# Expert matrices of a mixture-of-experts trunk loaded whole into two neighbouring slots instead of in two halves

## The chip, the cores and the metric

The kernel runs on one core of a Trainium2 chip. The metric is the device time of one execution in microseconds (us). The core has TensorE (PE, matrix products), VectorE (DVE), ScalarE (ACT), GpSimd (POOL) and SyncE (SP); SP only issues DMAs here. Sixteen DMA engines carry what the core reads and writes.

## What is computed

A trunk of two layers over 512 tokens of width 1024, all in float32. Layer 0 mixes tokens with a forgetting attention, layer 1 with a causal pooling; each is followed by a mixture of 32 experts, of which a token uses two. Every sub-layer has its RMS norm and is modulated by a vector that comes from `c` and the matrices `ada_w`. What matters here is the expert part:

```python
def grouped_moe(h, router_w, router_bias, w1, w3, w2):
    ...
    e_idx = top_k(where(e_mask, sel, -inf), 2)   # two experts of the best group
    ...
    def expert_block(args):
        xb, e = args
        return (silu(xb @ w1[e]) * (xb @ w3[e])) @ w2[e]
    ...
for i in range(2):
    mod = silu(c) @ ada_w[i] + ada_b[i]
    x = x + gt_m * mixer_i(modulate(rmsnorm(x), sh_m, sc_m))
    x = x + gt_f * grouped_moe(modulate(rmsnorm(x), sh_f, sc_f), ...)
```

Each of the 32 experts has w1 and w3 (1024 x 512) and w2 (512 x 1024): three matrices of 2 MB (2 x 1,048,576 bytes), so 192 MB a layer.

## The kernel before

**Passes.** A layer's experts run in 13 passes of up to 128 token places. A pass holds one to four experts: 2, 2, 4, 2, 2, 2, 1, 4, 2, 2, 3, 2, 4 in the order of passes 0 to 12 (`PASSES`). Which real expert stands on which place is found by routing; only three places (`STATIC`) have a fixed expert, the two of pass 0 and one of the two of pass 1 (number 31). For a pass, `step` in `experts` multiplies the gathered tokens by w1 (`up`, L1150), gathers the tokens of the next pass (L596), multiplies by w3 (`up` again), forms the gate, turns it (L1164), and multiplies by w2 (`down`, L1181; `down_half`, L1190, in the last pass). The products of the pass before are added into the tokens beside w1 (`combine`, L1198 and L1199). `up` and `down` run over slices of the contraction outside (8 slices j for w1 and w3, 4 for w2) and over the experts of the pass inside. TensorE's order in the expert part is the order in which the code stands (`ORDERED`).

**The stream of weights.** All large weights (the `ada_w` pieces in front, the attention's matrices, the experts of both layers) stand in one list. `Stream.pump` takes the next item as long as a slot is free and issues its load on SP's queue (L113); SP waits there, in the order of the list, until the slot's last reader is through and a completion counter is free. `done` returns slots and calls `pump`. Three tile pools make up the slots, 8 KB in each of the 128 partitions, 1 MB in all: `ring` with 5 (`FRONT_SLOTS`), `side` with 3, added during the attention, and `ring2` with 8, added when the attention is over. From there on 16 slots stand.

**Halves.** Every expert matrix comes as two loads of 1 MB (`expert_src`, `expert_items`): the first half of its contraction rows, then the second, where the loads of all experts of a pass for w1 and w3 stand ahead of those for w2. In a half each partition gets one row of 8 KB. In the last pass w2 is halved by columns instead, in rows of 2 KB. `up` and `down` call `done` after each half, so a half's slots go back when TensorE has used it.

**Routing.** Twelve loads of pass 0 and four of expert 31 (its w1 and w3) are issued before routing is known. Every other load needs its expert's number: SP reads it with `values_load` (L1047) before each load, and the list doesn't go on until the numbers are there.

**Front.** The modulation vector of layer 0 needs eight pieces of `ada_w`, multiplied at L273; the next stage starts with its result.

Of the kernel before, what the change touches and what calls it, by code (L numbers as in the profile page):

```python
# [10 lines left out]
F32 = mybir.dt.float32  # L11
# [30 lines left out]
WINDOWS = (2, 4, 8, 16)  # L42
FRONT_SLOTS = 5
SIDE_SLOTS = 3
MORE_SLOTS = 8
# [33 lines left out]
class Stream:  # L79


    def __init__(self, nc):
        self.nc = nc
        self.pools = []
        self.free = []
# [8 lines left out]
    def add(self, key, src, ready=lambda: True):  # L94
        self.items.append((key, src, ready))

    def pump(self):
        while self.next < len(self.items) and any(self.free):
            i = next(i for i, n in enumerate(self.free) if n)
            key, src, ready = self.items[self.next]  # L100
            if not ready():
                return
            self.next += 1
            self.free[i] -= 1
            t = self.pools[i].tile([128, 2048], F32, name="w", tag="w")
            src = src() if callable(src) else src
            n = 1
# [6 lines left out]
            self.live[key] = (t, i)  # L114

# [10 lines left out]
def kernel(  # L126
# [26 lines left out]
    stream = Stream(nc)  # L153
    stream.add_pool(ring, FRONT_SLOTS)

# [11 lines left out]

    def expert_src(w, l, k, a, columns):
# [6 lines left out]
        n = v.shape[1] // 2  # L175
        return v[:, :, 512 * a:512 * a + 512] if columns else v[:, n * a:n * a + n, :]

    def expert_items(l, i):

        items = []  # L180
        for name, w in (("w1", exp_w1), ("w3", exp_w3), ("w2", exp_w2)):
            for a in range(2):
                for ab, k in enumerate(PASSES[i][0]):
                    items.append((name == "w2", k < NE - STATIC, (name, l, i, ab, a), w, k))
        for cols, ranked, key, w, k in sorted(items, key=lambda v: v[:2]):
            stream.add(key, partial(expert_src, w, l, k, key[4], cols and i == len(PASSES) - 1),
                       lambda ranked=ranked: not ranked or l in order)
# [55 lines left out]
    own = const.tile([128, 4], F32, name="own")  # L243
# [623 lines left out]
    for side in range(2):  # L867
        r, p = slice(2 * side, 2 * side + 2), slice(64 + 2 * side, 66 + 2 * side)
# [89 lines left out]

    side = ctx.enter_context(tc.tile_pool(name="side", bufs=SIDE_SLOTS, side="right"))
    stream.add_pool(side, SIDE_SLOTS)  # L960
    stream.pump()
# [382 lines left out]
    ready = {}  # L1344
# [212 lines left out]
```

## Time and profile before

| | us |
|---|---|
| median of 3 runs | 1379.99 (1376.43 to 1381.18) |
| profiled execution, its own time | 1378.45 |
| its span, first to last instruction | 1376.9 |
| TensorE busy | 1223.6 (89%) |
| DMA queue of the weights, share of 16 engines | 86.4% |
| VectorE, ScalarE, GpSimd busy | 649.4, 376.3, 130.8 |
| expert loads, 384 of 1 MB, issue to landing | 19.8 each |

The span stands in two halves of the same build: attention until about 375 us and experts of layer 0 from there to about 870, pooling to about 905 and experts of layer 1 to the end. The mean granted TensorE clock is 0.968 of full speed. A busy TensorE is not yet the bound: where it and the DMA engines are both busy all the time, the waits say which of them the other waits for. "MB" of a DMA row of the profile is a million bytes; a load of 1 MB in the table above has 1,048,576.

### The profile page before, as it was taken

The numbers are of one execution on the slowest core, as the hardware profiler recorded it, in microseconds if no ns is written. First come the engines' busy times: TensorE is split into PE (matmuls) and PEld (weight loads), VectorE is DVE, ScalarE is ACT, GpSimd is POOL, SyncE is SP. The second block draws the span as 40 slices with busy tenths as digits, with TensorE's granted clock in tenths as the row PEclk, the third lists the DMA queues.
The fourth block names the chain that finished last, engine by engine and source line by source line (L and its number), as shares of the span: only waits on it lengthen the run. The fifth ranks groups of instructions, "written<-read, shape, count | busy, mean of one in ns | idle before, by whom it ended". The sixth has DMA issues, their size and how long they took to land. (4 is left out here: it accounts for less than half of the span.)

```text
span 1376.9 us, 19137 instructions
## 1 busy us (share of the span) xinstructions
PE 1223.6 (89%) x6872; PEld 633.6 (46%) x6873; DVE 649.4 (47%) x1284; ACT 376.3 (27%) x754; POOL 130.8 (10%) x90
## 2 busy tenths in 40 slices
PE   5689999988899999999998787899999998998874
PEld 2467677756544344443442224644344453443321
DVE  2787777787743333432332324744343342333314
ACT  3545555633621111111110013721111111111003
POOL 1322333425100000000000010100000000000000
PEclk9799999999999999999999898999999999999998
DMA  8755655758599999999999999479999999999995
GB/s 325 242 184 184 218 190 182 258 190 318 222 368 395 420 420 419 421 419 419 420 420 419 413 405 412 174 286 384 422 420 420 420 420 419 420 419 420 418 407 191
DMA packets 91145, 479.30 MB, mean 348 GB/s; under 512 B 12470, under 2 KB 25910, under 8 KB 37764
## 3 DMA queue, kind: packets, MB, share of 16 engines
q1 hardware_dynamic: 89920, 475.33, 86.4%
q10 hardware_dynamic: 496, 1.81, 0.4%
q8 instruction: 57, 0.93, 0.3%
q0 software_dynamic: 624, 0.84, 0.2%
q14 instruction: 48, 0.39, 0.1%
HBM read 475.55 MB, written 2.38 MB: 347 GB/s over the span
## 5 line engine op out<-in xcount | busy, mean ns | idle before, releaser
L1150 PE MATMUL h<-w,xgT 128*32 128x512 f32 (+2 forms) x2240 | 385.5, 598 | 13.9 <-DMA w<-in_exp_w_dram 13.3
L1150 PEld LDWEIGHTS h<-w,xgT 128*32 128x32 f32 (+2 forms) x2240 | 117.5, 123 | 249.1 <-issue 214.4
L1181 PE MATMUL y<-w,gT 128*32 128x512 f32 (+2 forms) x992 | 189.7, 617 | 22.8 <-DMA w<-in_exp_w_dram 16.2
L1200 DVE TENSOR_TENSOR xs<-xs,t 128x512 f32<-128x512 f32 x100 | 64.1, 681 | 138.4 <-PE t L1199 138.4
L1181 PEld LDWEIGHTS y<-w,gT 128*32 128x32 f32 (+2 forms) x992 | 55.7, 127 | 137.9 <-issue 97.9
L1171 DVE SCALAR_TENSOR_TENSOR y<-y,gs,gt 128x512 f32<-128x512 f32 x52 | 39.2, 754 | 157.0 <-PE y L1181 131.9
L711 POOL TENSOR_TENSOR wl<-w,wh 128x1024 fp32r<-128x1024 f32 x32 | 93.2, 2919 | 186.2 <-ACT wh L710 186.2
L1158 DVE TENSOR_TENSOR yl<-yl,h 128x512 f32<-128x512 f32 x26 | 17.9, 688 | 184.4 <-PE h L1150 171.5
L1141 ACT CAST yh<-y 128x512 fp32r<-128x512 f32 x52 | 30.5, 587 | 259.2 <-DVE y L1171 259.2
L1080 ACT ACTIVATE xgT<-t,modT 128x128 f32<-128x128 f32 x104 | 46.0, 458 | 190.4 <-PE t L1102 186.5
L311 DVE SCALAR_TENSOR_TENSOR lo<-w,cc,lo 128x2048 f32<-128x2048 f32 x28 | 80.1, 2859 | 0.4
L701 PE MATMUL h<-hi,wh 128*128 128x512 f32 x168 | 70.2, 418 | 0.0
L1156 ACT ACTIVATE yl<-h 128x512 f32<-128x512 f32 x26 | 15.6, 598 | 189.2 <-PE h L1150 189.2
L596 PE MATMUL c<-x,P 128*128 128x512 f32 x192 | 59.2, 431 | 9.1 <-DVE P L1113 9.1
L701 PE MATMUL h<-hi,wl 128*128 128x512 f32 x168 | 66.5, 396 | 0.0
L701 PE MATMUL h<-lo,wh 128*128 128x512 f32 x168 | 66.4, 395 | 0.0
L824 ACT ACTIVATE sb<-y,mx 128x128 f32<-128x128 f32 (+3 forms) x64 | 33.8, 528 | 75.7 <-DVE mx L823 73.3
L596 PE MATMUL c<-lo,P 128*128 128x512 f16 x192 | 51.3, 391 | 0.0
L1085 DVE TENSOR_SCALAR yh<-c 128x512 f32<-128x512 f32 x24 | 16.6, 692 | 68.2 <-PE c L596 68.2
L596 PEld LDWEIGHTS c<-x,P 128*128 128x128 f32 x192 | 37.0, 195 | 21.5 <-issue 12.1
L1142 DVE TENSOR_TENSOR yl<-y,yh 128x512 fp32r<-128x512 f32 x52 | 35.8, 688 | 19.7 <-ACT yh L1141 19.7
L1198 PE MATMUL t<-yh,PT 128*128 128x512 f32 x100 | 42.4, 424 | 2.6 <-DVE xs L1200 2.6
(361 smaller groups left out, 1739.2 us busy)
## 6 DMA issues: line engine op xcount, KB each, us to landing
w<-in_exp_w_dram SPq DMA_DIRECT2D x384, 1024.0 KB, 19.8
w<-in_ada_w_dram SPq DMA_DIRECT2D x48, 1024.0 KB, 5.2
w<-in_attn_w_in_dram SPq DMA_DIRECT2D x12, 1024.0 KB, 7.6
w<-in_attn_w_o_dram SPq DMA_DIRECT2D x4, 1024.0 KB
xs<-in_x_dram SPq DMA_DIRECT2D x1, 2048.0 KB
out_dram<-x SPq DMA_DIRECT2D x4, 512.0 KB
gt<-row ACTq DMA_DIRECT2D x2, 512.0 KB
w<-in_pool_w_dram SPq DMA_DIRECT2D x1, 1024.0 KB
```

Source lines behind the costliest of these rows:

```text
L311: V.scalar_tensor_tensor(ada_sum["s"], w, cc[:, j:j + 1], ada_sum["s"], op0=OP.mult, op1=OP.add)
L596: PE.matmul(pc[hf], P[part][:, t], R[("hi", "lo")[part]][:, t, 4 * hf:4 * hf + 4, :].rearrange("p j d -> p (j d)"), start=t == 0 and part ...
L701: PE.matmul(ps, a, b, start=first and n == 0, stop=last and n == 2)
L711: G.tensor_sub(lo, w, hi.bitcast(F32))
L824: S.activation(sb[:, h, :n], ps[:, :n], AF.Exp, bias=mx[:, h:h + 1], accum_out=ls[:, h:h + 1])
L1080: S.activation(xT[:, j, :], ps, AF.Identity, scale=A, bias=sh)
L1142: V.tensor_sub(yl, y, yh.bitcast(F32))
L1150: PE.matmul(ps[r, :], xT[:, j, r], wt(name, ab, j, None), start=j == 0, stop=j == 7)
L1171: V.scalar_tensor_tensor(py, py, gs, R["gt"][:, 512 * hf:512 * hf + 512], op0=OP.mult, op1=OP.mult)
L1181: PE.matmul(py[hf][r, :], gT[:, j, r], wt("w2", ab, j, hf), start=j == 0, stop=j == 3)
L1198: PE.matmul(ps, PT[:, t, :], y[0], start=True, stop=False)
L1200: V.tensor_add(xs[:, t, hs], xs[:, t, hs], ps)
```

## The change

The three pools are replaced by three tiles of 6, 3 and 8 slots, which the kernel divides itself. The slots of a tile are paired, 0 with 1, 2 with 3 and so on; the third slot of `side` has no neighbour, so 17 slots make 8 pairs and one odd one. Expert matrices are loaded whole, 16 KB in each partition, into a pair that is free (the pair that has been free longest). Exceptions are all three matrices of pass 0 and w2 of the last pass, which stay in halves as before (`shares` is 2), as do the items that are no expert weights. A load of 1 MB takes a free slot whose neighbour is in use or missing, if there is one. `done` gives back a whole matrix only after its second half is used. The expert part so has 212 loads (172 of 2 MB, 40 of 1 MB) where it had 384. The scratch memory that the program reserves for descriptors written by GpSimd is 8192 bytes instead of the default; this is what the build is given, no instruction changes by it.

```diff
-FRONT_SLOTS = 5
+FRONT_SLOTS = 6
 SIDE_SLOTS = 3
 MORE_SLOTS = 8
...
 class Stream:
-    def add_pool(self, pool, n):
-        self.pools.append(pool)
-        self.free.append(n)
+    def add_room(self, tile, n):
+        for i in range(n):
+            self.slots.append(dict(tile=tile, at=2048 * i, since=0))
+        own = self.slots[-n:]
+        for i, slot in enumerate(own):
+            slot["mate"] = own[i ^ 1] if i ^ 1 < n else None
...
+    def room(self, large):
+
+        def free(slot):
+            return slot is not None and slot["since"] is not None
+
+        if large:
+            pairs = [(a, a["mate"]) for a in self.slots if free(a) and free(a["mate"]) and a["at"] < a["mate"]["at"]]
+            return min(pairs, key=lambda p: max(p[0]["since"], p[1]["since"]), default=None)
+        return min(((a,) for a in self.slots if free(a)), key=lambda p: (free(p[0]["mate"]), p[0]["since"]), default=None)
 
     def pump(self):
-        while self.next < len(self.items) and any(self.free):
-            i = next(i for i, n in enumerate(self.free) if n)
-            key, src, ready = self.items[self.next]
-            if not ready():
+        while self.next < len(self.items):
+            key, src, large, ready = self.items[self.next]
+            own = self.room(large)
+            if own is None or not ready():
                 return
             self.next += 1
-            self.free[i] -= 1
-            t = self.pools[i].tile([128, 2048], F32, name="w", tag="w")
+            for slot in own:
+                slot["since"] = None
+            t = own[0]["tile"][:, own[0]["at"]:own[0]["at"] + 2048 * len(own)]
...
     def done(self, *keys):
         for key in keys:
-            self.free[self.live.pop(key)[1]] += 1
+            self.count += 1
+            for slot in self.live.pop(key)[1]:
+                slot["since"] = self.count
         self.pump()
...
-    ring = ctx.enter_context(tc.tile_pool(name="ring", bufs=FRONT_SLOTS))
+    ring = ctx.enter_context(tc.tile_pool(name="ring", bufs=1))
...
-    stream.add_pool(ring, FRONT_SLOTS)
+    stream.add_room(ring.tile([128, FRONT_SLOTS * 2048], F32, name="w"), FRONT_SLOTS)
...
+    def shares(i, name):
+
+        return 2 if i == 0 or (i, name) == (len(PASSES) - 1, "w2") else 1
...
-            for a in range(2):
+            for a in range(shares(i, name)):
...
             def done(name, a):
-                stream.done(*[(name, l, i, ab, a) for ab in range(len(PASSES[i][0]))])
+                if shares(i, name) == 2 or a:
+                    stream.done(*[(name, l, i, ab, a if shares(i, name) == 2 else 0) for ab in range(len(PASSES[i][0]))])
...
-    nc = bacc.Bacc("TRN2", target_bir_lowering=False, num_devices=1)
+    nc = bacc.Bacc("TRN2", target_bir_lowering=False, num_devices=1, dynamic_dma_scratch_size=8192)
```

The instructions of PE, DVE, ACT and POOL keep their order, but for one exchange of neighbours at the end of the attention. SP's queue changes, and what the matmuls wait for.

SP's queue, where layer 0's last loads that need no routing (expert 31) and the first that do stand; `numi` is the routing's result. Before:

```order
L113 DMA w_3185<-in_exp_w1_dram 128x2048 [waits DMAHW5_49]
L113 DMA w_3187<-in_exp_w1_dram 128x2048 [waits DMAHW6_49]
L113 DMA w_3189<-in_exp_w3_dram 128x2048 [waits DMAHW7_49]
L113 DMA w_3191<-in_exp_w3_dram 128x2048 [waits DMAHW0_49]
L1047 TENSOR_LOAD numi_3282 [waits DMAHW3_49,DMAHW4_49,DMAHW2_49,DMAHW5_49,DMAHW0_49,DMAHW6_49,DMASW2_49,DMAHW7_49,DVE_49,Pool_49]
L1047 ISA x2
L113 ISA
L113 DMA w_3284<-in_exp_w1_dram 128x2048 [waits DMAHW1_49,PE_49]
L1047 TENSOR_LOAD numi_3282
L1047 ISA x2
L113 ISA
L113 DMA w_3296<-in_exp_w1_dram 128x2048 [waits DMAHW2_49,PE_49]
```

After (`w_72` is the tile of 6 slots, `w_side` that of 3, `w_more` that of 8):

```order
L128 DMA w_more_3108<-in_exp_w2_dram 128x2048 [waits DMAHW2_49]
L128 DMA w_more_3108<-in_exp_w2_dram 128x2048 [waits DMAHW3_49]
L128 DMA w_more_3108<-in_exp_w1_dram 128x4096 [waits DMAHW4_49]
L128 DMA w_more_3108<-in_exp_w3_dram 128x4096 [waits DMAHW6_49]
L1068 TENSOR_LOAD numi_3203 [waits DMAHW3_49,DMAHW2_49,DMAHW4_49,DMAHW1_49,DMAHW5_49,DMAHW0_49,DMAHW6_49,DMASW2_49,DMAHW7_49,DVE_49,Pool_49]
L1068 ISA x2
L128 ISA
L128 DMA w_72<-in_exp_w1_dram 128x4096 [waits DMAHW7_49,PE_49]
L1068 TENSOR_LOAD numi_3203
L1068 ISA x2
L128 ISA
L128 DMA w_side_2664<-in_exp_w3_dram 128x4096 [waits DMAHW5_49,DMAHW0_49,PE_49]
```

A load of 128x4096 replaces two of 128x2048, and one reading of the expert's number serves it; the first load after routing still waits for the first half of pass 0's w1 (PE), the next for w3's first half.

TensorE's queue at w2 of pass 2, the first with four experts, whose loads are the DMAHW counters. Before:

```order
L1181 MATMUL y<-w,gT 32x512 [waits DMAHW1_49,DVE_49]
L1181 MATMUL y<-w,gT 32x512 [waits DMAHW2_49]
L1181 MATMUL y<-w,gT 32x512 [waits DMAHW3_49]
L1181 MATMUL y<-w,gT 32x512 [waits DMAHW4_49]
L1181 MATMUL y<-w,gT 32x512 x12
L1181 MATMUL y<-w,gT 32x512 [waits DMAHW5_49]
L1181 MATMUL y<-w,gT 32x512 [waits DMAHW6_49]
L1181 MATMUL y<-w,gT 32x512 [waits DMAHW7_49]
L1181 MATMUL y<-w,gT 32x512 [waits DMAHW0_49]
L1181 MATMUL y<-w,gT 32x512 x12
```

After:

```order
L1202 MATMUL y<-w_more,gT 32x512 [waits DMAHW3_49,DVE_49]
L1202 MATMUL y<-w_more,gT 32x512 [waits DMAHW4_49]
L1202 MATMUL y<-w,gT 32x512 [waits DMAHW5_49]
L1202 MATMUL y<-w_more,gT 32x512 [waits DMAHW6_49]
L1202 MATMUL y<-w_more,gT 32x512 x2
L1202 MATMUL y<-w,gT 32x512
L1202 MATMUL y<-w_more,gT 32x512 x3
L1202 MATMUL y<-w,gT 32x512
```

The first four matmuls now wait for the four whole matrices, and no later one waits; before, the second half of the matrices had its waits after 16 matmuls.

SP's queue at the start of the program, the `ada_w` pieces that the modulation of layer 0 needs. Before:

```order
L223 DMA xs_69<-in_x_dram 128x4x1024
L113 DMA w_73<-in_ada_w_dram 128x2048
L113 DMA w_75<-in_ada_w_dram 128x2048
L113 DMA w_77<-in_ada_w_dram 128x2048
L113 DMA w_79<-in_ada_w_dram 128x2048
L113 DMA w_81<-in_ada_w_dram 128x2048
L113 DMA w_237<-in_ada_w_dram 128x2048 [waits DMAHW2_49,PE_49]
L113 DMA w_243<-in_ada_w_dram 128x2048 [waits DMAHW3_49,DMAHW0_49,PE_49]
L113 DMA w_249<-in_ada_w_dram 128x2048 [waits DMAHW4_49,DMAHW1_49,PE_49]
L617 DMA adab_139<-in_ada_b_dram 128x6x8
```

After:

```order
L244 DMA xs_69<-in_x_dram 128x4x1024
L128 DMA w_72<-in_ada_w_dram 128x2048 x6
L128 DMA w_72<-in_ada_w_dram 128x2048 [waits DMAHW2_49,DMAHW0_49,PE_49]
L128 DMA w_72<-in_ada_w_dram 128x2048 [waits DMAHW3_49,DMAHW1_49,PE_49]
L638 DMA adab_136<-in_ada_b_dram 128x6x8
```

Six instead of five pieces go without a wait for TensorE, and the two others wait for one slot earlier each.

## Rows read from the trace of the kernel before

**Rows 1.** The page's part 2: forty slices of the span, 34.4 us each.

```profile
PE   5689999988899999999998787899999998998874
...
DMA  8755655758599999999999999479999999999995
...
GB/s 325 242 184 184 218 190 182 258 190 318 222 368 395 420 420 419 421 419 419 420 420 419 413 405 412 174 286 384 422 420 420 420 420 419 420 419 420 418 407 191
```

**Rows 2.** The page's part 6, then SP's waits: total us, times, longest.

```profile
w<-in_exp_w_dram SPq DMA_DIRECT2D x384, 1024.0 KB, 19.8
...
SPq L113 <- DMA w<-in_exp_w_dram: 345.1, 248, 2.9
...
SPq L113 <- PE h L1150: 71.4, 35, 7.0
```

**Rows 3.** DMA view: windows 1000:1100 (8 KB rows), 5:7 (4 KB), 1340:1350 (2 KB).

```profile
DMA packets 5758, 41.99 MB, mean 420 GB/s; under 512 B 637, under 2 KB 637, under 8 KB 637
...
DMA packets 200, 0.82 MB, mean 410 GB/s; under 512 B 0, under 2 KB 0, under 8 KB 200
...
DMA packets 1895, 3.77 MB, mean 377 GB/s; under 512 B 59, under 2 KB 59, under 8 KB 1894
```

**Rows 4.** PE timeline (start, us, group), then window: busy us by engine, PEclk, DMA share, GB/s.

```profile
478.99 7.62 PE L1150 MATMUL h<-w,xgT 128*64 128x512 f32 x32
...
606.29 7.07 PE L1150 MATMUL h<-w,xgT 128*32 128x512 f32 x64
...
478.99:606.29 127.30, 126.03 (x545) 58.82 (x544) 47.86 (x91) 21.03 (x40) 0.00 (x0) 1.00 1.01 420
```

**Rows 5.** Passes 2 and 7: PE timeline, a window of it, SP's issues.

```profile
464.60 4.49 PE L1181 MATMUL y<-w,gT 128*32 128x512 f32 x36
...
473.02 3.62 PE L1181 MATMUL y<-w,gT 128*32 128x512 f32 x26 [1.45 <-DMA w<-in_exp_w_dram]
...
637.40 5.29 PE L1181 MATMUL y<-w,gT 128*32 128x512 f32 x26 [1.45 <-DMA w<-in_exp_w_dram]
...
637.40:640.80 3.40, 3.40 (x16) 0.79 (x20) 0.00 (x0) 0.00 (x0) 0.00 (x0) 0.50 1.02 422
...
609.98 8.36 SPq L113 DMA_DIRECT2D w<-in_exp_w_dram  x8
```

**Rows 6.** Pass 0 of layer 0: PE timeline, then SP's issues.

```profile
376.90 1.94 PE L1150 MATMUL h<-w,xgT 128*64 128x512 f32 x8 [0.30 <-ACT xgT L1080]
...
378.96 3.65 PE L1150 MATMUL h<-w,xgT 128*64 128x512 f32 x16
...
383.05 3.65 PE L1150 MATMUL h<-w,xgT 128*64 128x512 f32 x16
...
387.21 1.94 PE L1150 MATMUL h<-w,xgT 128*64 128x512 f32 x8
...
390.14 3.65 PE L1150 MATMUL h<-w,xgT 128*64 128x512 f32 x16
...
400.93 3.65 PE L1181 MATMUL y<-w,gT 128*64 128x512 f32 x16 [0.62 <-DVE gT L1166]
...
384.45 25.08 SPq L113 DMA_DIRECT2D w<-in_exp_w_dram  x12
```

**Rows 7.** DMA view of 384 to 412, GB/s in 40 slices of 0.7 us.

```profile
GB/s 0 0 199 257 257 456 363 363 433 421 421 398 445 386 433 421 433 398 433 445 410 398 421 456 410 421 410 456 421 398 410 375 316 351 351 398 410 386 421 410
```

**Rows 8.** Windows (columns as in rows 4) from the start of each expert stage.

```profile
384.00:432.00 48.00, 46.92 (x231) 21.39 (x227) 15.32 (x30) 10.55 (x19) 0.00 (x0) 1.00 0.96 378
...
904.00:952.00 48.00, 46.92 (x225) 20.79 (x225) 15.42 (x33) 9.69 (x17) 0.00 (x0) 1.00 0.94 374
```

**Rows 9.** PE timeline, front of the program.

```profile
30.34 1.06 PE L273 MATMUL c<-w,crep 128*32 128x512 f32 x8 [1.38 <-DMA w<-in_ada_w_dram]
```

**Rows 10.** PE timeline, last pass of layer 1.

```profile
1336.55 3.62 PE L1150 MATMUL h<-w,xgT 128*32 128x512 f32 x26 [1.47 <-DMA w<-in_exp_w_dram]
...
1348.01 4.98 PE L1190 MATMUL y<-w,gT 128*32 128x512 f32 x26 [1.61 <-DMA w<-in_exp_w_dram]
```

More of the change, by code (lines that the diff above doesn't have):

```diff
@@ L83, in __init__ @@
         self.nc = nc
-        self.pools = []
-        self.free = []
+        self.slots = []
         self.items = []
@@ L88, in __init__, with add @@
         self.live = {}
[L90 to L95 removed]
+        self.count = 0
+    def add_room(self, tile, n):
[4 more added lines that the diff above has]
+            slot["mate"] = own[i ^ 1] if i ^ 1 < n else None
+    def add(self, key, src, large=False, ready=lambda: True):
+        self.items.append((key, src, large, ready))
+    def room(self, large):
[5 more added lines that the diff above has]
+        return min(((a,) for a in self.slots if free(a)), key=lambda p: (free(p[0]["mate"]), p[0]["since"]), default=None)
     def pump(self):
[L98 to L101 removed]
+        while self.next < len(self.items):
+            key, src, large, ready = self.items[self.next]
+            own = self.room(large)
+            if own is None or not ready():
                 return
             self.next += 1
[L104 to L105 removed]
+            for slot in own:
+                slot["since"] = None
+            t = own[0]["tile"][:, own[0]["at"]:own[0]["at"] + 2048 * len(own)]
             src = src() if callable(src) else src
@@ L113, in pump @@
             self.nc.sync.dma_start(dst, src)
-            self.live[key] = (t, i)
+            self.live[key] = (t, own)
     def get(self, key):
@@ L181, in expert_items @@
         for name, w in (("w1", exp_w1), ("w3", exp_w3), ("w2", exp_w2)):
-            for a in range(2):
+            for a in range(shares(i, name)):
                 for ab, k in enumerate(PASSES[i][0]):
                     items.append((name == "w2", k < NE - STATIC, (name, l, i, ab, a), w, k))
-        for cols, ranked, key, w, k in sorted(items, key=lambda v: v[:2]):
-            stream.add(key, partial(expert_src, w, l, k, key[4], cols and i == len(PASSES) - 1),
+        for second, ranked, key, w, k in sorted(items, key=lambda v: v[:2]):
+            n = shares(i, key[0])
+            stream.add(key, partial(expert_src, w, l, k, key[4], n, second and i == len(PASSES) - 1), n == 1,
                        lambda ranked=ranked: not ranked or l in order)
@@ L957, in xgT @@
         return mt.tile([128, 8, 128], F32, name="xgT", tag="xgT", bufs=2)
-    side = ctx.enter_context(tc.tile_pool(name="side", bufs=SIDE_SLOTS, side="right"))
-    stream.add_pool(side, SIDE_SLOTS)
+    side = ctx.enter_context(tc.tile_pool(name="side", bufs=1, side="right"))
+    stream.add_room(side.tile([128, SIDE_SLOTS * 2048], F32, name="w_side"), SIDE_SLOTS)
     stream.pump()
@@ L1004 @@
     fstack.close()
-    ring2 = ctx.enter_context(tc.tile_pool(name="ring2", bufs=MORE_SLOTS))
-    stream.add_pool(ring2, MORE_SLOTS)
+    ring2 = ctx.enter_context(tc.tile_pool(name="ring2", bufs=1))
+    stream.add_room(ring2.tile([128, MORE_SLOTS * 2048], F32, name="w_more"), MORE_SLOTS)
     stream.pump()
@@ L1214, in get @@
             def get(name, ab, j, hf):
+                n = shares(i, name)
                 if hf is None:
-                    return stream.get((name, l, i, ab, j // 4))[:, 512 * (j % 4):512 * (j % 4) + 512]
-                a, at = (hf, 512 * j) if i == len(PASSES) - 1 else (j // 2, 1024 * (j % 2) + 512 * hf)
-                return stream.get((name, l, i, ab, a))[:, at:at + 512]
+                    j, at = j % (8 // n) * 512, j * n // 8
+                elif i == len(PASSES) - 1:
+                    j, at = 512 * j, hf
+                else:
+                    j, at = 1024 * (j % (4 // n)) + 512 * hf, j * n // 4
+                return stream.get((name, l, i, ab, at))[:, j:j + 512]
             def done(name, a):
-                stream.done(*[(name, l, i, ab, a) for ab in range(len(PASSES[i][0]))])
+                if shares(i, name) == 2 or a:
+                    stream.done(*[(name, l, i, ab, a if shares(i, name) == 2 else 0) for ab in range(len(PASSES[i][0]))])
             return get, done
```

6 lines of the change are left out of this document (3 added, 3 removed).

## The prediction

> **What bounds the kernel now.** I read the page's forty slices first. From slice 14 to 25 and from 29 to 39, of 34.4 us each, the DMA engines are busy in all tenths and move 405 to 422 GB/s [rows 1]; these are the two expert stages. There TensorE is nearly as busy, so the question is which of the two waits. SP's waits and the issue table answer it: an expert load of 1 MB (1,048,576 bytes, called a piece here) lands 19.8 us after its issue, and SP waits 248 times for an earlier one of them, 345.1 us in all, against 35 times and 71.4 us for w1 or w3 matmuls that still hold a slot [rows 2]. Eight pieces are in flight, and at 420 GB/s [rows 3] one takes 1.0486 MB / 420 GB/s = 2.497 us. A layer's experts are 192 pieces, 479 us. TensorE needs 127.30 us for four passes in a row [rows 4], 31.8 us a pass whatever number of experts it has, so 13 x 31.8 = 414 us. The stream of weights sets the end, with some 65 us of slack on TensorE over a layer; but the slack isn't everywhere. From 478.99 to 606.29 TensorE works without a gap [rows 4], because these four passes hold only 2, 2, 2 and 1 experts (42 pieces, 105 us): there TensorE is the slow one and the stream runs as far ahead as the slots let it. What matters of this change is therefore three things: microseconds per piece, when a slot can be filled again, and whether TensorE is late just where the slots are all taken.
>
> **Part 1, longer rows: less time per piece.** The trace has rows of 2, 4 and 8 KB at full load: 377, 410 and 420 GB/s [rows 3]. One of 16 engines so takes 86.9 ns for 2 KB, 159.8 for 4 KB and 312.1 for 8 KB. The step from 4 to 8 KB costs 152.3 ns, from 2 to 8 KB 225.2 ns; carried on, 16 KB cost 312.1 + 304.6 = 616.7 ns or 312.1 + 300.3 = 612.4 ns, which is 425 or 428 GB/s. No row of 16 KB is in the trace. I take 426 GB/s, 2.461 us a piece, a gain of 0.036 us. Bounds: 430 (2.439 us) above; below, nothing (420 is what these engines do), or even a loss down to the 410 of the 4 KB rows. Whole matrices are all pieces of a layer but the 16 loaded before routing is known (pass 0 and four of expert 31) and the 8 of the last pass's w2, which keep their 2 KB rows: 168 pieces x 0.036 = 6.0 us a layer, 12 in all, if nothing is given back.
>
> The Trainium skill has a rule for this price, in "DMA: Bandwidth & Descriptors", section "Why small descriptors are slow (HBM only)": about three cycles for each packet on top of one per 32 bytes. By it 8 KB take 256 + 3 and 16 KB 512 + 3 cycles, 0.58% less per byte, and a layer would gain about 168 x 0.014 = 2.4 us. By the same rule 2 KB would lose 3.5% against 8 KB, where the rows show 10% [rows 3], so the trace has a larger fixed cost than the rule, and I go by the rows.
>
> **Part 2, the start of a layer: neighbours must both be free.** Before, each half of a matrix that TensorE has used lets two pieces go. By the trace [rows 6], w1 of pass 0 is 32 matmuls, 8 from 376.90, 16 from 378.96 and the first 8 of those from 383.05: its halves are used by 380.8 and 384.9, those of w3 by 389.07 and 393.72, those of w2 by 404.6 and 408.2. SP's twelve issues from 384.45 to 409.5 [rows 6] follow these times, so 8 pieces (20 us) are on their way by 395 and the next come at 404.6: the stream hardly pauses. After, a whole load needs a pair. Reading the slots off the order of the changed program, pass 0's first half of w1 frees a pair, its second half lies beside the odd slot and beside a slot of w3 and frees none, w3's halves free one pair each, w2's first half one and its second two. So 6 pieces are out by 393.7, not 8: from 385.4 (the first data come 1.0 us after the first issue [rows 7]) they last 6 x 2.461 to 400.2, and the fourth pair comes at 404.5 + 1.0, a pause of 5.3 us; later, with two pairs freed at the end of pass 1's w3, I find another of 0.5. The old stream pauses too: 384 to 432 moved 378 GB/s [rows 8], 4.8 us short of 420, of which 1.4 passed before the first data; 3.4 were pauses. Layer 1 is alike (374 GB/s [rows 8], the same steps 520.6 us later). Extra pause: 5.8 - 3.4, about 2.3 us a layer; bounds 0 (the backlog lets later issues catch up) and 5.3.
>
> **Part 3, passes of four experts: TensorE starts them later.** The loop runs over the eighths of a matrix outside and over the experts inside, so the fourth matmul group already needs the fourth matrix. With halves, 26 matmuls, 3.62 us, were left when the last piece of pass 2's w2 landed at 473.02 [rows 5]; with whole matrices nearly all are left, 7.1 us (the 64 of 606.29 [rows 4]): 3.5 us more. It also waits in one stretch from about 465, and the granted clock fell to 0.50 for 3.40 us after the waits before 637.40 [rows 5], which lost 1.7 us; I add it (bounds 0 and 1.7). So pass 2 ends later by 2.3 (part 2) - 32 x 0.036 (part 1) + 3.5 + 1.7 = 6.3 us. The stretch to 606.29 has no gap, so pass 7 begins its w1 6.3 us late. There the slots are all taken: pass 7 has four experts, its w1 and w3 are 16 pieces. Before, SP issued the eight pieces of its w2 from 609.98 on, when the first half of w1 was used [rows 5]; they landed last at 637.40, so their stream began 8 x 2.497 earlier, at 617.4. After, w1 comes free only whole, at 606.29 + 7.07 + 6.3 = 619.7, and the stream goes on at 620.7, having been ready sooner: 3.3 us later than before. All that the stream had gained is lost at this place. From there 78 pieces of whole matrices follow in the layer, 2.8 us of gain. Four of these passes hold 2, 2, 3 and 2 experts (135 us of DMA against 127), so the stream leads again. A layer: +3.3 - 2.8 = +0.5 us; two layers +1.0.
>
> **Part 4, the rest.** In front a sixth slot lets the sixth piece of the first ada weights go without waiting for a slot, and the next ones one slot earlier; TensorE waited 1.38 us for the last of them at 30.34 [rows 9] with the stage behind it: -1.0 (bounds 0 and -1.4). The last pass's w1 and w3 come whole: its last w3 matmuls start later by 3.5 us than the 26 from 1336.55, but the next stop is the landing of w2's first half at 1348.01 [rows 10], which has the same place in the stream; without that cover it would be 3.5 us. SP issues 172 loads fewer; eight that need an expert's number take it 8.36 us [rows 5], less than their 20 us of data, so nothing is gained. The instructions of TensorE, VectorE, ScalarE and GpSimd stay in their order, and the smaller scratch costs nothing that a row shows.
>
> **The sum** is 1378.45 (the profiled execution, 1376.9 of span and 1.55 around it) + 1.0 - 1.0 = 1378.4; the median of the runs lies 1.5 above it, so 1379.9. I take 1379.0, between them.
>
> **Rivals.**
> *The lumps are hidden* (faster). If the stream catches up at the layer's start and TensorE's lateness is absorbed before pass 7, the 12 us stay: 1379 - 12 - 1 = 1366; with only the clock's 1.7 and the start's 2.3 gone, pass 7's w2 starts 0.7 us earlier than before, a layer gains 3.5, and 1371 comes out; with everything as I have it but 430 GB/s, 1374. For it: TensorE's slack of 65 us a layer. Against it: the gapless stretch [rows 4] lies just between the two passes.
> *The rate doesn't rise, the lumps stay* (slower). If a 16 KB row travels as two of 8 KB, or 420 is a limit that no row length moves, pass 2 ends 7.5 us late, pass 7's w2 starts at 621.9, and each layer ends 4.5 us late: 1379 + 9 - 1 = 1387. The change would then not do what it says on the wire. It decides from 423 GB/s down. For it: the step from 4 to 8 KB brought only 10 GB/s.
> *The curve flattens.* From 2 to 4 and from 4 to 8 KB the rate rose by 33 and by 10 GB/s [rows 3]. If the next step is again a third, 3, then 423 GB/s come out (2.479 us, 0.018 less), and a layer ends 4.5 - 110 x 0.018 = 2.5 us late, since 32 + 78 pieces gain: 1379 + 5 - 1 = 1383. The three cycles of the Trainium skill ("DMA: Bandwidth & Descriptors", "Why small descriptors are slow (HBM only)") would give 0.014 us a piece and 1384.
>
> **How the numbers follow.** A measurement of this kernel tells 0.3%, 4.1 us, from no change. My forecast, 1379 with 1374 to 1384 around it: 0.44 (0.08 of it faster, 0.36 the same). Lumps hidden: 0.25, all faster, 1366 to 1374. No rise: 0.19, all slower but 0.01, 1384 to 1389. Flattening: 0.12, half the same and half slower, 1381 to 1386. Faster 0.33, the same 0.43, slower 0.24. The range from 1367 to 1388 leaves out the fastest of the hidden lumps, a loss of rate, and what I haven't thought of.
>
> **What would show it.** The GB/s of a window inside a stage (1000 to 1100) tells part 1 at once: 426, 420 or between. Part 2 shows in 384 to 432 and 904 to 952 against [rows 8], as a pause near 400 to 405. Part 3 shows in TensorE's wait and clock before pass 2's w2, in the start of pass 7's w1 against 606.29, and in a hole of the DMA between that w1 and its w2. Part 4 shows in the wait at 30.34. The forecast fails if pass 7 starts no later than before, or if the windows show 420.

## The result and the profile after

The changed kernel takes 1391.74 us (median of 7 runs, 1386.95 to 1397.22) against 1379.99 of the kernel before: 1.0078 of its time, 95% interval 1.0053 to 1.0103. It is slower by some 11 us. The prediction, 1379 with a range from 1367 to 1388, expected no difference that can be told; the measured time lies above the range. The profiled execution has a span of 1389.3 us, 12.4 more than before.

Three views say where these 12.4 us are. First the slices of the page (GB/s of 40 slices, 34.7 us each; the row above is TensorE's granted clock in tenths), to hold against [rows 1]:

```profile
PEclk9799999998899899999999988999899998999987
...
GB/s 326 266 185 181 230 200 180 233 209 302 180 278 405 424 428 427 426 383 374 426 427 427 419 412 408 226 262 347 415 428 426 426 410 371 428 426 426 428 412 213
```

Beside it the DMA view of 1000 to 1100 us, which answers to the first of [rows 3]:

```profile
DMA packets 2926, 42.66 MB, mean 427 GB/s; under 512 B 322, under 2 KB 322, under 8 KB 322
```

Half as many packets, twice as long, 427 GB/s where 420 stood. Rows of 16 KB are faster, by what was forecast (426). But the slices show holes that weren't there: 383 and 374, 410 and 371 in the midst of each expert stage.

Second, how late the same matmul of TensorE starts, read off both PE timelines (w1 of the pass named):

| place | before | after | late by |
|---|---|---|---|
| layer 0, pass 0 | 376.90 | 383.30 | 6.40 |
| pass 2 | 442.21 | 448.68 | 6.47 |
| pass 3 | 478.99 | 494.02 | 15.03 |
| pass 7 | 606.29 | 620.84 | 14.55 |
| pass 8 | 645.04 | 662.41 | 17.37 |
| layer 1, pass 0 | 897.77 | 908.54 | 10.77 |
| pass 3 | 998.49 | 1016.99 | 18.50 |
| pass 7 | 1125.83 | 1143.79 | 17.96 |
| pass 8 | 1163.92 | 1186.88 | 22.96 |
| pass 12 | 1314.17 | 1331.34 | 17.17 |
| last matmul of w2 | 1361.72 | 1374.20 | 12.48 |

Three of these starts in the profile after, for passes 0, 3 and 7 of layer 0 (before: [rows 6] and [rows 4]):

```profile
383.30 2.01 PE L1171 MATMUL h<-w,xgT 128*64 128x512 f32 x8 [0.30 <-ACT xgT L1101]
...
494.02 0.64 PE L1171 MATMUL h<-w_side,xgT 128*64 128x512 f32 x1
...
620.84 0.62 PE L1171 MATMUL h<-w_more,xgT 128*32 128x512 f32 x1
```

So 6.4 us are lost **before the first expert**, 8.6 and 7.7 at pass 2 of each layer, 2.8 and 5.0 at pass 7, and 6.6 and 10.5 come back behind it. The attention's end was no term of the prediction.

Third, the places themselves. The attention's end: VectorE in the kernel before and after (start, us, group, and in brackets the idle time ahead and what ended it), then TensorE before and after.

```profile
316.24 2.12 DVE L407 TENSOR_TENSOR P<-rw,modT 128x256 f32<-128x256 f32 x1 [0.41 <-PE c L848]
318.28 2.58 DVE L410 TENSOR_TENSOR xgT<-rw,modT 128x256 f32<-128x256 f32 x1
320.89 0.60 DVE L412 TENSOR_REDUCE xgT<-xgT 128x32 f32<-128x256 f32 x1
321.40 2.22 DVE L885 TENSOR_TENSOR lo<-x,hi 128x512 fp32r<-128x512 f32 x1
...
323.64 2.33 DVE L311 SCALAR_TENSOR_TENSOR w<-w,cc 128x2048 f32<-128x2048 f32 x1
...
327.10 3.00 DVE L311 SCALAR_TENSOR_TENSOR w<-w,cc 128x2048 f32<-128x2048 f32 x1
```

```profile
316.03 2.06 DVE L428 TENSOR_TENSOR P<-rw,modT 128x256 f32<-128x256 f32 x1 [0.49 <-PE c L869]
318.02 4.45 DVE L332 SCALAR_TENSOR_TENSOR w<-w,cc 128x2048 f32<-128x2048 f32 x1
322.39 2.82 DVE L906 TENSOR_TENSOR lo<-x,hi 128x512 fp32r<-128x512 f32 x1
325.14 2.34 DVE L332 SCALAR_TENSOR_TENSOR w<-w,cc 128x2048 f32<-128x2048 f32 x1
327.40 0.41 DVE L431 TENSOR_TENSOR xgT<-rw,modT 128x256 f32<-128x256 f32 x1
327.85 0.58 DVE L433 TENSOR_REDUCE xgT<-xgT 128x32 f32<-128x256 f32 x1
```

```profile
321.59 0.38 PE L414 MATMUL c<-xgT,ones_f 128*128 128x32 f32 x2 [2.51 <-issue]
```

```profile
328.53 0.60 PE L435 MATMUL c<-xgT,ones_f 128*128 128x32 f32 x2 [9.67 <-issue]
```

L410 and L431 are the same instruction, the routing's set-up, on whose result the next matmul in TensorE's order waits. After, two pieces of the second layer's modulation (L332, 4.45 and 2.34 us) and a subtraction (L906, 2.82 us) stand ahead of it, and TensorE is idle for 9.67 us instead of 2.51. This is what the section on the change calls "one exchange of neighbours" and the prediction cost at nothing. By the traces it is more than that: three instructions of VectorE moved ahead of two, and one of GpSimd's (L711, after L732) behind three.

Pass 2's w2 on TensorE (to hold against [rows 5]), then windows of the two starts and of pass 7 (columns as in [rows 4]; the starts are those of [rows 8], shifted by how late pass 0 is), then SP's issues of the last four loads of pass 7's w2:

```profile
471.99 1.19 PE L1202 MATMUL y<-w_more,gT 128*32 128x512 f32 x4 [0.24 <-DVE gT L1187]
477.02 1.87 PE L1202 MATMUL y<-w,gT 128*32 128x512 f32 x2 [3.85 <-DMA w<-in_exp_w_dram]
481.93 1.08 PE L1202 MATMUL y<-w_more,gT 128*32 128x512 f32 x3 [3.04 <-DMA w_more<-in_exp_w_dram]
```

```profile
390.50:438.50 48.00, 46.92 (x231) 21.39 (x227) 15.33 (x31) 10.57 (x19) 0.00 (x0) 1.00 0.90 356
914.80:962.80 48.00, 46.93 (x225) 20.82 (x226) 15.42 (x33) 9.73 (x17) 0.00 (x0) 1.00 0.87 351
612.00:636.00 24.00, 23.78 (x136) 10.31 (x138) 9.45 (x17) 2.99 (x5) 0.00 (x0) 1.00 0.75 287
```

```profile
627.92 0.34 SPq L128 DMA_DIRECT2D w_more<-in_exp_w_dram  x1
629.08 0.34 SPq L128 DMA_DIRECT2D w<-in_exp_w_dram  x1
630.24 0.34 SPq L128 DMA_DIRECT2D w_more<-in_exp_w_dram  x1
631.41 0.34 SPq L128 DMA_DIRECT2D w_side<-in_exp_w_dram  x1
```

TensorE can do next to nothing of pass 2's w2 until the fourth matrix has landed at 481.9, and then runs it at half clock (1.08 us for matmuls that take 0.6 otherwise). The starts move 356 and 351 GB/s where 378 and 374 stood. And around pass 7's w1 (620.84 on) the stream moves 287 GB/s over 24 us, 24 x (427 - 287) / 427 = 7.9 us lost: its w2 is issued from 627.92, right after the w1 ends.

### The profile page after: what moved, and what is told of

It is laid out like the page before. It is cut to its first block, busy times and chain, and to the rows that moved or that the text cites. A ratio compares the mean times of both kernels' runs of the same rounds, so it can differ in the third digit from the quotient of the medians.

```text
span 1389.3 us, 18018 instructions
## 1 busy us (share of the span) xinstructions
PE 1226.2 (88%) x6872; PEld 633.7 (46%) x6873; DVE 647.9 (47%) x1284; ACT 376.0 (27%) x754; POOL 136.1 (10%) x90
## 4 chain that ended last, share of the span: by engine, by line
PE 54%; DVE 17%; DMA 17%; ACT 7%; issue 4%; SPq 1%; ACTq 0%; DVEq 0%
PE h L1171 21%; PE y L1202 10%; DMA w_more<-in_exp_w_dram 7%; DMA w<-in_exp_w_dram 6%; DVE lo L332 4%; PE c L617 4%; PE h L722 3%; PE t L1219 2%; DVE mx L844 2%; PE t L1220 1%; DMA w_side<-in_exp_w_dram 1%; DVE y L1192 1%; DVE yl L1163 1%; PE c L1220 1%; DMA w<-in_ada_w_dram 1%
## 5 line engine op out<-in xcount | busy, mean ns | idle before, releaser
L1171 PE MATMUL h<-w,xgT 128*32 128x512 f32 (+2 forms) x872 | 288.2, 606 | 11.2 <-DMA w<-in_exp_w_dram 10.8
L1171 PE MATMUL h<-w_more,xgT 128*32 128x512 f32 (+1 forms) x1056 | 278.3, 601 | 0.1
L1202 PE MATMUL y<-w_more,gT 128*32 128x512 f32 (+2 forms) x504 | 147.1, 672 | 18.6 <-DMA w_more<-in_exp_w_dram 16.1
L1202 PE MATMUL y<-w,gT 128*32 128x512 f32 (+1 forms) x408 | 126.1, 636 | 13.3 <-DMA w<-in_exp_w_dram 9.5
L1171 PE MATMUL h<-w_side,xgT 128*32 128x512 f32 (+1 forms) x312 | 133.6, 601 | 0.3 <-ACT xgT L1101 0.3
L1171 PEld LDWEIGHTS h<-w,xgT 128*32 128x32 f32 (+2 forms) x872 | 82.2, 128 | 99.6 <-issue 81.0
L1171 PEld LDWEIGHTS h<-w_more,xgT 128*32 128x32 f32 (+1 forms) x1056 | 77.2, 121 | 105.9 <-issue 103.6
L732 POOL TENSOR_TENSOR wl<-w,wh 128x1024 fp32r<-128x1024 f32 x32 | 98.6, 3085 | 185.5 <-ACT wh L731 185.5
L332 DVE SCALAR_TENSOR_TENSOR lo<-w,cc,lo 128x2048 f32<-128x2048 f32 x28 | 82.0, 2929 | 0.4
L1202 PEld LDWEIGHTS y<-w_more,gT 128*32 128x32 f32 (+2 forms) x504 | 41.2, 139 | 84.6 <-issue 58.8
L1202 PEld LDWEIGHTS y<-w,gT 128*32 128x32 f32 (+1 forms) x408 | 32.0, 128 | 58.0 <-issue 40.0
```

Source lines behind the costliest of these rows:

```text
L332: V.scalar_tensor_tensor(ada_sum["s"], w, cc[:, j:j + 1], ada_sum["s"], op0=OP.mult, op1=OP.add)
L732: G.tensor_sub(lo, w, hi.bitcast(F32))
L1171: PE.matmul(ps[r, :], xT[:, j, r], wt(name, ab, j, None), start=j == 0, stop=j == 7)
L1202: PE.matmul(py[hf][r, :], gT[:, j, r], wt("w2", ab, j, hf), start=j == 0, stop=j == 3)
```

## The experiments

Two theories stood against each other. **A**: four causes, each at its place: the order of VectorE (6.4 us), missing pairs at a layer's start, passes of four experts, and a slot that only halves can use. **B**: the expert stage waits for its weights in any case, so that a loss at one place is absorbed at the next, and what counts is a single one of them. The edits are of two kinds. The order of VectorE is restored by writing the last two ada pieces behind the routing's set-up:

```diff
-                if what == "ada":
+                if what == "ada" and u < 31:
                     piece = ada_piece(*key)
...
         R = route_open(0)
+        steps(ada_piece(*late[-2]), 1)
...
             out_close(acc[t], 0, t)
+            if t == 1:
+                ada = ada_piece(*late[-1])
+                steps(ada, 1)
```

and which passes come in halves is one condition in `shares` (w2 of the last pass is always in halves). Ratios are to the kernel before, on the same chip each, with their 95% interval:

| run | order restored | slots | in halves | median us | ratio |
|---|---|---|---|---|---|
| changed kernel | no | 17 | pass 0 | 1391.74 | 1.0078 (1.0053 to 1.0103) |
| e1, the old pools | no | 17 | all | 1382.63 | 1.0012 (0.9994 to 1.0031) |
| e2 | yes | 17 | pass 0 | 1387.81 | 1.0048 (1.0031 to 1.0065) |
| e3 | yes | 17 | all | 1373.13 | 0.9939 (0.9923 to 0.9956) |
| e4 | yes | 17 | 0, 2, 7, 12 | 1369.71 | 0.9921 (0.9903 to 0.9939) |
| e5 | yes | 17 | 0, 1, 2, 7, 12 | 1363.69 | 0.9874 (0.9851 to 0.9896) |
| e6 | yes | 17 | all but 8 to 11 | 1367.00 | 0.9909 (0.9889 to 0.9930) |
| e7 | as before by itself | 16 | all | 1383.16 | 1.0010 (0.9991 to 1.0030) |
| e8 | yes | 17 | 0, and w2 of 2 and 7 | 1375.08 | 0.9956 (0.9939 to 0.9974) |
| e9 | no | 17 | 0, 1, 2, 7, 12 | 1371.83 | 0.9926 (0.9905 to 0.9946) |
| e10 | yes | 17 | 0, 1, 2, 7 | 1361.14 | 0.9850 (0.9824 to 0.9876) |
| e11 | yes | 17 | 0, 1, 2, 7, 10, 12 | 1365.56 | 0.9885 (0.9861 to 0.9910) |

**e1, the sixth slot in the old kernel.**

```diff
-FRONT_SLOTS = 5
+FRONT_SLOTS = 6
...
-    nc = bacc.Bacc("TRN2", target_bir_lowering=False, num_devices=1)
+    nc = bacc.Bacc("TRN2", target_bir_lowering=False, num_devices=1, dynamic_dma_scratch_size=8192)
```

> The old kernel with three pools and halves throughout, and only the sixth front slot (and the smaller scratch that it needs). Theory A: the sixth slot alone makes VectorE do the last two ada pieces before the routing's set-up, and TensorE waits some 9.7 us there instead of 2.5; the old kernel gets about 6.4 us slower, 1386 against 1380. Rival B: the loss at the end of the attention comes from the new ring or from the whole matrices; then this run stays within 2 us of before.

The time is the old kernel's within the interval, 1.7 us above it by the medians. That is rival B's number, but not by its reason: the trace has theory A's wait, without any new ring or whole matrix:

```profile
335.19 0.60 PE L414 MATMUL c<-xgT,ones_f 128*128 128x32 f32 x2 [9.52 <-issue]
```

The slot therefore also brings something, about as much as the order takes; e3 and e7 show what.

**e2, VectorE's order restored in the changed kernel** (the first diff above, alone).

> The changed kernel, with the last two ada pieces written behind the routing's set-up, so that VectorE has the order that it had before. Theory A: it gains the 6.4 us that the traces lie apart between 308 and 330 us, 1385 against 1391.7. Rival B: the wait of TensorE is only covered otherwise and the expert stage waits for its weights anyway, so under 2 us are gained.

TensorE's wait is back to its old length,

```profile
321.08 0.38 PE L435 MATMUL c<-xgT,ones_f 128*128 128x32 f32 x2 [2.49 <-issue]
```

and layer 0's experts start at the old time. 1.0048 against 1.0078 is 0.3%, 4 us, between the theories, and the intervals overlap. The profiled executions lie 6.9 us apart, and in their expert stages both fall behind the kernel before by the same (6.1 us in the changed kernel, 5.8 in e2), so they show nothing that is absorbed there. e9 measures the same edit in a better kernel.

**e3, all matrices in halves.**

```diff
-        return 2 if i == 0 or (i, name) == (len(PASSES) - 1, "w2") else 1
+        return 2
```

> As e2, but every expert matrix still in two halves: seventeen slots divided by the kernel, VectorE's order restored, no whole matrix. Theory A: the new ring by itself costs nothing, so before's time or up to 2 us less for the extra slot: 1378 to 1380. Rival B: the ring's division costs something of its own (the slots' order, waits of SP), then 1383 or more. The window 1000 to 1100 should move 420 GB/s as before, not 427.

8 us faster than before, more than theory A allowed: the ring with seventeen slots isn't neutral, it is the gain. The starts of the two stages show a part of it (shifted as above; [rows 8] had 378 and 374), some 2 us each:

```profile
388.60:436.60 48.00, 46.91 (x231) 21.36 (x227) 15.29 (x30) 10.55 (x19) 0.00 (x0) 1.00 0.98 398
903.60:951.60 48.00, 46.92 (x226) 20.79 (x225) 15.42 (x33) 9.65 (x17) 0.00 (x0) 1.00 0.97 392
```

Inside the stage it moves the old 419 to 420 GB/s. From e3 to e2 nothing changes but that matrices are whole: 1373 to 1388. Whole matrices everywhere cost 15 us, faster rows included.

**e4, passes of four experts in halves.**

```diff
-        return 2 if i == 0 or (i, name) == (len(PASSES) - 1, "w2") else 1
+        return 2 if i in (0, 2, 7, 12) or (i, name) == (len(PASSES) - 1, "w2") else 1
```

> As e2, with the passes of four experts (2, 7 and 12) in halves as well, the others but pass 0 whole. Theory A (the loss in the expert stage is the late start of TensorE in passes 2 and 7 and the stream that waits for pass 7's w1): the steps of 8 and 3 us there vanish, a layer loses some 2 us at its start and gains some 2 behind pass 7; 1376 to 1380. Rival B (the loss is the pause at a layer's start, where pairs are missing): the time stays near e2's 1385.

18 us faster than e2, and below theory A's range. The step at pass 2 doesn't vanish, though: from the start of a stage to w3 of pass 3, e4 still falls 4.2 us (layer 0) and 3.8 us (layer 1) behind the kernel before, where e2 falls 8.0 and 8.1 behind. The hole at pass 7 is closed. The window 606 to 630 in e4, then in e2:

```profile
606.00:630.00 24.00, 23.78 (x153) 9.94 (x154) 8.28 (x13) 2.37 (x4) 0.00 (x0) 1.00 1.01 419
```

```profile
606.00:630.00 24.00, 23.78 (x142) 10.30 (x144) 8.74 (x14) 2.98 (x5) 0.00 (x0) 1.00 0.75 287
```

**e5, pass 1 in halves too.** The same line as in e4:

```diff
+        return 2 if i in (0, 1, 2, 7, 12) or ...
```

> As e4 (1369.7), with pass 1 in halves as well, so that the first loads after routing need single slots and no pairs. In e4 the end of pass 2's w2 still stands 4.2 us behind the old kernel in layer 0 and 3.8 in layer 1, in e3 (all halves) 4.7 and 2.0 ahead of it. Theory A: the pause of the stream at a layer's start, where pairs are missing, makes this, and it is carried to the layer's end; the step at pass 2 turns to some -4 us and the time falls by 6 to 12 us, to 1358 to 1364. Rival B: the stream is ahead of TensorE in passes 3 to 6 in any case, so the pause is absorbed there: 1368 to 1370.

6 us faster than e4, the near end of theory A's range. The windows of the starts, in e4 and then in e5 (like e3's):

```profile
386.00:434.00 48.00, 46.92 (x230) 21.37 (x227) 15.32 (x31) 10.50 (x19) 0.00 (x0) 1.00 0.89 355
900.90:948.90 48.00, 46.92 (x226) 20.79 (x225) 15.42 (x33) 9.67 (x17) 0.00 (x0) 1.00 0.97 392
```

```profile
387.50:435.50 48.00, 46.92 (x231) 21.35 (x227) 15.30 (x29) 10.57 (x19) 0.00 (x0) 1.00 0.98 399
899.60:947.60 48.00, 46.92 (x226) 20.79 (x225) 15.43 (x33) 9.67 (x17) 0.00 (x0) 1.00 0.97 393
```

In layer 0 the pause is real, goes with this edit, and 2.7 us of it are left at the layer's end in the profiled executions. In layer 1 it was gone in e4 already, with the passes of four in halves (e2 moves 351 GB/s there, e4 392). What halves of pass 1 bring in that layer is therefore not this pause, and no run shows what it is.

**e6, whole matrices in passes 8 to 11 alone.**

```diff
+        return 2 if i not in (8, 9, 10, 11) or ...
```

> As e5, with passes 3 to 6 in halves too: whole matrices are left in passes 8 to 11 alone (54 pieces of 168 a layer). Theory A: TensorE is the slow one in passes 3 to 6 (a pass each 31.8 us without a gap), so the faster rows bring nothing there: within 1.5 us of e5. Rival B: the stream is the bound there as well, so 42 pieces of 0.04 us are lost, 1.7 us a layer: 3 to 4 us slower than e5.

3.3 us slower than e5: theory B's number, but the intervals overlap a little, and the profiled executions lose it in layer 1 alone (3.1 us; layer 0's stage is as long in both). Between 500 and 600 TensorE has no gap, and the stream has none either. The window in e6, then in e5:

```profile
500.00:600.00 100.00, 98.92 (x419) 46.17 (x416) 38.29 (x71) 16.57 (x32) 0.00 (x0) 1.00 1.01 420
```

```profile
500.00:600.00 100.00, 99.04 (x440) 45.46 (x437) 35.93 (x66) 15.77 (x30) 0.00 (x0) 1.00 1.01 424
```

One price of whole matrices in passes 3 to 6 was in neither theory. In e5 TensorE waits at the start of pass 3's w1 for the second whole matrix, and then works at half clock (1.12 us for matmuls that take 0.6 otherwise):

```profile
481.78 1.12 PE L1175 MATMUL h<-w_side,xgT 128*64 128x512 f32 x1 [2.76 <-DMA w_side<-in_exp_w_dram]
```

From w1 of pass 3 to w1 of pass 7 it needs 133.6 and 130.6 us in the two layers, in e6 127.4 and 127.9, in the kernel before 127.3. e5 makes this good later in the layer. No run has only pass 3's w1 in halves.

**e7, five front slots and halves.** The new ring with the old number of slots:

```diff
-FRONT_SLOTS = 6
+FRONT_SLOTS = 5
...
+        return 2
```

> The ring that the kernel divides, but with five front slots as before (sixteen in all) and halves throughout. VectorE has the old order here without any edit. Theory A: e3's gain of 8 us over the old kernel is the seventeenth slot; without it the time is the old kernel's, 1379 to 1382. Rival B: it is the division itself (which slot a load takes); then 1373 to 1375 stays.

The old kernel's time within the interval: the way the ring is divided costs nothing and brings nothing. The seventeenth slot is worth 1.0010 - 0.9939, some 10 us, once VectorE's order is kept.

**e8, only w2 of passes 2 and 7 in halves.**

```diff
+        return 2 if i == 0 or (name == "w2" and i in (2, 7)) or ...
```

> As e2 (1387.8), with only w2 of passes 2 and 7 in halves; w1 and w3 of these passes stay whole. It divides the 18 us between e2 and e4. Theory A: both parts of the argument on passes of four experts hold; TensorE's late start at w2 costs about 3.5 + 1.7 us a time, so most of the step at pass 2 beyond e4's goes and about half of the 18 us, to 1377 to 1381, while the hole of the stream between pass 7's w1 and w2 stays. Rival B: the whole w1 that keeps pass 7's slots is what matters: 1385 to 1388.

By the ratios 12.7 of the 18 us between e2 and e4 come from w2, more than the half that theory A gave it. The hole at pass 7, which theory A expected to stay, is mostly gone:

```profile
606.00:630.00 24.00, 23.78 (x148) 10.08 (x150) 8.30 (x13) 2.52 (x5) 0.00 (x0) 1.00 0.95 380
```

It isn't pass 2's w2 that closes it: TensorE comes to pass 7 almost as late as in e2 (6.8 us behind the kernel before, against 7.8). By the issues it is pass 7's own w2. Two of its halves find single slots and are issued at 611.91 and 616.79 (the first of the two in its row), ahead of the end of w1 at 620.2; in e2 the first whole one is issued at 621.16, when w1 ends.

```profile
611.91 0.34 SPq L128 DMA_DIRECT2D w_side<-in_exp_w_dram  x1
616.79 3.77 SPq L128 DMA_DIRECT2D w_more<-in_exp_w_dram  x2
```

At pass 2 the halves let TensorE end w2 earlier, 2.2 us behind the kernel before at w1 of pass 3 where e2 is 8.3 behind. But there it waits for the stream, and at pass 3's w3 it is 6.9 us behind, against 7.8 in e2:

```profile
485.01 1.11 PE L1175 MATMUL h<-w_more,xgT 128*64 128x512 f32 x1 [2.76 <-DMA w_more<-in_exp_w_dram]
```

So the late start at pass 2's w2 was for the most part not what held layer 0 up. No run halves only one of the two w2.

**e9, e5 without the restored order.** Against the changed kernel:

```diff
+        return 2 if i in (0, 1, 2, 7, 12) or ...
```

> e5 (0.987 of before) with the order of VectorE that the sixth slot brings, that is without the edit of e2. It asks what the order costs in a kernel whose expert stage isn't held up elsewhere. Theory A: the 6.4 us of TensorE's longer wait are paid in full: 1370 against 1363.7 (0.992 of before). Rival B: after and e2 lie only 4 us apart (1.0078 and 1.0048 of before), so part of it is absorbed later: 1366 to 1368.

8 us slower than e5 by the medians, 0.52% by the ratios (7 us); TensorE's wait is 9.68 us again:

```profile
331.76 0.61 PE L435 MATMUL c<-xgT,ones_f 128*128 128x32 f32 x2 [9.68 <-issue]
```

Theory A: the order is paid in full. That the medians of e2 gave back only 4 us of it is within the intervals, which allow 6; its profiled execution gave back 6.9.

**e10, the last pass's w1 and w3 whole.**

```diff
+        return 2 if i in (0, 1, 2, 7) or ...
```

> e5 with w1 and w3 of the last pass whole (w2 of it stays in halves by columns). Theory A, as the prediction had it: TensorE starts them up to 3.5 us later, but the landing of w2's first half covers that; the time stays e5's or falls by up to 1.3 us (32 pieces of 0.04 us). Rival B: w2's loads wait for the whole w1, as in pass 7, and nothing comes behind to make it good: 3 us or more slower than e5, 0.990 of before or more.

0.2% faster than e5 by the ratios, with intervals that overlap: the last pass loses nothing that can be told by whole w1 and w3, as the prediction had it. This kernel has the lowest median of the case, 1361.14 us, 1.5% under the kernel before.

**e11, pass 10 (three experts) in halves.**

```diff
+        return 2 if i in (0, 1, 2, 7, 10, 12) or ...
```

> e5 with pass 10 (three experts) in halves as well. Theory A: three whole matrices make a smaller lump than four (TensorE waits for the third), and the pass lies where the stream leads, so halves bring nothing and 18 pieces a layer lose 0.04 us each: 0 to 2 us slower than e5. Rival B: the lump of three costs TensorE and slots as in passes 2 and 7: 2 to 4 us faster than e5.

1.9 us slower than e5 by the medians (1.5 by the ratios), within theory A's range and within the uncertainty. Halves bring no gain here that can be told; a small one is not excluded.

## Why the prediction was wrong

The profiled execution is 12.4 us longer than before. 6.4 of them are an order of instructions that part 4 put at nothing, and 6.1 are the expert stages, which the sum had at 1.0; the front, put at -1.0, came to nothing.

**What failed first: part 4, "the instructions ... stay in their order".** The listing of the order had an exchange at the attention's end, and the prediction put no price on it. Its price was to be had from rows of before: an ada piece takes VectorE 2.3 to 3 us, two of them ahead of L410 are some 5 to 6, and the matmul that L410 feeds was already waited for (2.5 us). It measured 6.4 (7 in e9). And the sixth slot is its cause: e1 has it with the old pools, e7 without that slot hasn't. Likely the two pieces are loaded earlier and are then placed ahead of the set-up when the order is made; no run shows this step itself.

**Part 4, the front: -1.0 forecast, +0.9 measured.** TensorE's timeline after shows why:

```profile
27.39 1.07 PE L294 MATMUL c<-w,crep 128*32 128x512 f32 x8 [1.00 <-DMA w<-in_ada_w_dram]
30.35 1.94 PE L294 MATMUL c<-w,crep 128*32 128x512 f32 x8 [1.90 <-DMA w<-in_ada_w_dram]
```

The last piece is used at 30.35, as before at 30.34 [rows 9]: the DMA engines were already carrying 420 to 422 GB/s from 12 to 28 us in the kernel before, so an earlier issue moved nothing. TensorE only waited in two pieces and came out at half clock, 1.94 us for the work of 1.06. By 60 us it had been made good.

**Part 4 left out what the slot is for.** e3 against e7 puts the seventeenth slot at some 10 us, and the timelines of the two place 8.9 of them in the expert stages. The prediction looked for its worth in front only. What it brings in the changed kernel no run shows: by the code the sixth front slot makes the eighth pair there, and what has no neighbour, so that no whole matrix fits it, is the third slot of `side`.

**Part 1 was right.** 427 GB/s against 426, 420 before. By the Trainium skill's three cycles a packet ("DMA: Bandwidth & Descriptors", "Why small descriptors are slow (HBM only)") 422 would have come out, an estimate worked out from 420. The trace bears out a larger cost per row.

**Part 2 was right in kind, and somewhat short.** Forecast 2.3 us more pause a layer; the windows say 48 x (427 - 356) / 427 = 8.0 against the 4.8 of before in layer 0, 3.2 more, and 48 x (427 - 351) / 427 = 8.54 against 5.26 in layer 1, 3.3 more. In layer 1 it goes with halves in the passes of four (e4), in layer 0 with halves in pass 1 (e5).

**Part 3 had the places and the hole at pass 7; its sums were too small, and its reason for pass 2 was not the main one.** Pass 2 was to end 6.3 us late and ended 8.6 and 7.7 late, with the waits (3.85 and 3.04) and the half clock that it named. The stream of pass 7's w2 was to be held up by the whole w1, and was: SP issued its loads from 627.92, as the w1 ended. Set against the later start of the stage, w2's data came 627.92 + 1.0 - 6.4 - 617.4 = 5.1 us late where 3.3 were forecast. Behind it 6.6 us came back in layer 0 and 10.5 in layer 1, measured on TensorE, whose own late start at w2 (some 5 us) is in these numbers; the stages as wholes lost 10.77 - 6.40 = 4.4 and 12.48 - 10.77 = 1.7 us, 6.1 together, where the sum had 1.0.

Part 3 took pass 2's lateness for TensorE's late start at w2, with the stream ahead again behind it. The runs put most of it on the stream. From the start of a stage to w3 of pass 3, TensorE falls behind the kernel before by:

| run | whole up to pass 6 | layer 0 | layer 1 |
|---|---|---|---|
| e6 | none | -4.2 | -2.0 |
| e5 | passes 3 to 6 | 1.8 | 0.2 |
| e4 | pass 1 too | 4.2 | 3.8 |
| e8 | w1 and w3 of pass 2 too | 7.3 | 7.1 |
| e2 | w2 of pass 2 too | 8.0 | 8.1 |

The whole w2, for which the prediction charged 3.5 + 1.7 us, adds 0.7 and 1.0. (These are single executions, and e8 and e2 also differ from e4 in passes 7 and 12, which can bear on layer 1.) Two of its smaller readings are off by tenths and move nothing: pass 0's w2 is used by 408.0, not 408.2, and the layers lie 520.9 us apart, not 520.6 (897.77 - 376.90).

**The premise about passes 3 to 6 was half right.** In the changed kernel they have no gap on TensorE and so hand its lateness on to pass 7, as the table of places shows (15.03 to 14.55, 18.50 to 17.96). But the stream isn't ahead at their start: e4, e5 and e8 wait for it at pass 3's w1. Lumps cost more than was charged: from e2 to e4, 18 us where the prediction's terms for them come to some 8 (its +1.0 against the -12 without them, less 2 x 2.3 for the pairs).

**Put together**, by ratios of 1380 us: the seventeenth slot -10 (e3 and e7), whole matrices everywhere +15 (e2 and e3), VectorE's order +4 (the changed kernel and e2) to +7 (e9 and e5). That is +9 to +12, and +11 was measured. With +4 the three are steps of one chain from e7 to the changed kernel, so that their sum comes out by itself; that the order's +7 was measured apart, in e9, is the check. The whole matrices' +15 is 24 of pairs and lumps (18 from passes of four, 6 from pass 1) less the 9 by which e5 is ahead of e3. The faster rows of the passes that are left whole in e5 account for 2 x 96 pieces x 0.041 us = 7.9 of these 9, by 420 and 427 GB/s. The forecast's rival of a slower kernel, in which the rate doesn't rise, wasn't the cause.

## What to carry to other kernels

In this kernel larger transfers gain by their bytes and lose at a few places, where they let a consumer start later or let a buffer go later; find those places and keep them in small pieces (here four of 13 passes and w2 of a fifth), and the gain is left. Price every line of difference in an engine's order, however short: ask which waiting engine stands behind the moved instruction. And a buffer more can change the order in which instructions are placed, so read the order again after any change of a ring.

## What the runs showed of the hardware

Rows of 16 KB move 427 GB/s, against 420, 410 and 377 for 8, 4 and 2 KB in these traces (427 and 420 over 100 us, 410 over 2 us, 377 over 10).

TensorE's granted clock can fall without a gap right ahead of it. In e1 it worked without idle time from 116 us on, 32 matmuls of two columns each among it (117.2 to 119.2), and then had a mean of 0.60 of its full 2.4 GHz over four us, for the most part at its lower level of 1.2 GHz, and did 16 matmuls in them. The kernel before did the same work there at 1.00, 22 matmuls. The windows of the kernel before, then of e1:

```profile
116.00:120.00 4.00, 4.00 (x47) 3.43 (x46) 2.68 (x7) 2.13 (x4) 0.00 (x0) 1.00 0.18 72
120.00:124.00 4.00, 4.00 (x22) 3.35 (x21) 3.50 (x5) 1.32 (x3) 0.58 (x1) 1.00 0.26 52
```

```profile
116.00:120.00 4.00, 4.00 (x48) 3.40 (x47) 2.56 (x7) 2.26 (x6) 0.00 (x0) 0.98 0.21 82
120.00:124.00 4.00, 4.00 (x16) 3.23 (x15) 2.17 (x1) 0.55 (x2) 0.59 (x1) 0.60 0.24 38
```

This fall put e1 1.6 us further behind. The profiled executions differ in how many there are in the attention: the changed kernel's has none, e1 falls behind by such a step at four places, and at three of them (120, 224 and 306 us) its windows show a granted clock below 1.00 (0.60, 0.70 and 0.69). The one at 224 has a wait of 2.27 us shortly ahead of it, the two others have none. How much of the scatter of the times (1377.64 to 1389.99 in e1) they make was not measured.
